# Block 2's projections with tokens on partitions in 512-column products, and a fixed time per product in the ordering estimate

## The chip, the core and the metric

The kernel runs on one core of one Trainium2 chip. The metric is the device time of one execution in microseconds; of three runs of the kernel before the median is 1619.11 us (1617.6 to 1622.94). Everything is in float32: a product of two matrices is either taken in full float32, or both operands are split into a leading part (type float32r) and the rest, and three products of the parts are added.

## The reference

Two blocks follow each other on 256 tokens of width 1024.

```
x = first_block(x, mem, ...)      # mixer (conv + chunked recurrence), cross attention, 16-expert MoE, final norm
for l in range(2):                # second_block, on the tokens x and on 256 context tokens
    h, hc = modulated_norm(x), modulated_norm(ctx)
    na_q, na_k, na_v, cq, ckv, k_rope, dq, dk, dv, z, gm = split(h @ w_in[l])      # and the same of hc
    na_q, na_k, dq, dk = rms_norm per head of 64 columns          # dq, dk rotated afterwards
    mq = rms_norm(cq) @ w_uq[l];  k_nope, mv = split(rms_norm(ckv) @ w_ukv[l])
    o_na, o_mla, o_diff = three attentions
    y = sum_i sigmoid(g_i) * ((o_i * silu(z_i)) @ w_br[l][i])
    x = x + gate * (y @ w_out[l])                                 # ctx likewise, in layer 0 alone
```

## The kernel before

The program is one stream of instructions for each engine, written out by a planner in Python. Every part of the computation is a generator (a fiber); `run` always continues the fiber whose next step can begin first by an estimate of when each engine is free (`self.E`), and among equals the one of the higher priority. The estimate of a product's time is made in `_pe` (L346). What stands on an engine stands in that order for good: each engine works through its stream in order and waits where an operand isn't there. The program is built three times; each of the last two builds takes the order of the weight loads from the build before it.

Weights come in units of 1024 values a partition (512 KB) by a DMA from SP into the large tiles. ScalarE writes the leading part (`wh`, 128x1024), VectorE the rest (`wl`), and the products of a unit then use both. Names of tiles in a profile: `wh`, `wl` the split weights, `t` a fiber's tile, `p` a PSUM bank of 512 float32 columns, `csts` the constants (a product with these at L370 is a transposition), `X` the tokens. In `p<-wh,t` the weights move through TensorE and the tokens are stationary: this is a product with tokens on partitions. `p<-t,wh` is the other kind, with features on partitions.

PSUM has eight banks; `pg`, `pa`, `po` (L176) limit how many of these the products of projections, the short products and the attention outputs may hold at once: 6, 4 and 3.

Block 2 has its keys, values and queries (attention branches `na` and `diff`), the last latent keys and values (`w_ukv`) and the final matrix (`w_out`) through `gemm_t` (L679): blocks of 256 columns, the weights of a unit being four rows of 128 by 256 columns, and the two token tiles of a stream side by side in one PSUM bank. Three products for each row of 128, token tile and block:

```
self.mm(o, hi.k(k)[:, ts], w.hi[:, k - u], m == 0 and k == 0, False)
self.mm(o, hi.k(k)[:, ts], w.lo[:, k - u], False, False)
self.mm(o, lo.k(k)[:, ts], w.hi[:, k - u], False, m == 1 and k == kt - 1)
```

`ev_qk` takes keys or queries out of PSUM (square, sum per head, 1/rms once for both blocks of 256 columns, scale, rotate, transpose), `ev_vals` the values, `evac` in `out` the last product (times the gate, onto the residual, and in layer 1 out by a DMA). Block 1 has products of this kind with 512 columns already, in `gemm_x`.

In the middle of the kernel is the router of block 1's experts. Its logits are two groups of twelve short products (`t,wrh` and `t,wrl`, into 20 partitions); ScalarE copies them out (`t<-p,cols 20x256`), TensorE transposes them (`csts,t` into 20 columns), and a chain of short VectorE operations makes the routing. Near it `prepare` writes sixteen tables of the attention's bias into DRAM, by DMAs that are issued from ScalarE's own stream (L949, `toep<-in_na_rpb_dram`).

Of the kernel before, what the change touches and what calls it, by code (L numbers as in the profile page):

```python
# [26 lines left out]
# ---------------------------------------------------------------- layout of the packed small operands  # L27
# [72 lines left out]
# ---------------------------------------------------------------- program order  # L100
# [5 lines left out]
class Fiber:  # L106
# [20 lines left out]
class Tiles:  # L127
    """[128, n, w] held as tiles of per entries each."""
# [12 lines left out]
class Core:  # L141
    """Emits the program. Each part of the computation is a generator; run() interleaves them by an
    estimate of when the engines are free, so that one part's products fill another's waits."""
# [18 lines left out]
    GR, GP = 4, 0.5  # L162
# [40 lines left out]
    # ---- generators  # L203
# [47 lines left out]
    # ---- memory  # L251
# [28 lines left out]
    def alloc_t(self, n, w, dt=F32):  # L280
        """[128, n, w] in as many tiles as it takes."""
# [25 lines left out]
    def wlimit(self, phase):  # L307
        """the phase's share of the large tiles for weights; what a smaller share gives back is used once it is empty."""
# [11 lines left out]
    def soon(self, eng="pe"):  # L320
        """other parts first, if what comes would hold up the engine."""
# [16 lines left out]
    # ---- engines  # L338
# [7 lines left out]
    def _pe(self, cycles, rows, par=1.0):  # L346
        """the array runs at its full clock in a tick that follows one with enough columns; par: products side by side."""
# [5 lines left out]
        self._op("pe", cycles * (0.4167 if self.hot else 0.8333) / par)  # L353
# [8 lines left out]
    def mm(self, out, lhsT, rhs, start, stop, par=1.0):  # L362
        n, m = self._n(rhs), self._n(lhsT)
        self._pe(max(n, 2 * m) if rhs.dtype == F32R else max(4 * n, 4 * m), lhsT.shape[0], par)
# [53 lines left out]
    def rsqrt(self, ss, inv_n, n):  # L418
        """1/sqrt(ss*inv_n + EPS) for a [128, n] tile; 1/sqrt(ss) without inv_n."""
# [18 lines left out]
    def hilo(self, hi, lo, src, after=None):  # L438
        """Exact split of src: hi carries its leading bits, lo the rest."""
# [4 lines left out]
    # ---- weights  # L444
# [17 lines left out]
    def _slot(self):  # L462
        """a large tile for weights: the one that was given back first."""
# [10 lines left out]
    def _pump(self):  # L474
        """loads ahead of the products, in the recorded order, as far as the buffers allow."""
# [3 lines left out]
    def splitter(self):  # L479
        """splits ahead of the products; hi: the leading bits of the unit's weights, lo: the rest."""  # L480
# [26 lines left out]
    def wget(self, name, lead, k0, k1, c0, c1, plain=False):  # L507
        """the weights [k0*128:k1*128, c0:c1], [128, k, c]: split, or plain as they are."""
# [66 lines left out]
    def gemm_w(self, name, lead, K, c0, c1, hi, lo, evac):  # L575
        """out[feature, token]: evac(i, psum [128, 2, 256]) for each 256 columns."""
# [19 lines left out]
    def gemm_x(self, name, lead, K, c0, c1, hi, lo, evac, cw=512):  # L596
        """out[token, feature]: evac(i, [psum of tokens 0-127, psum of tokens 128-255], n)."""
# [2120 lines left out]
```

## Time and profile before

| | |
|---|---|
| three runs, median (lowest, highest) | 1619.11 us (1617.6, 1622.94) |
| profiled execution: span of its instructions | 1620.1 us |
| TensorE matmuls, busy | 1581.4 us (98%), 11642 instructions |
| TensorE weight loads, busy | 1333.1 us (82%) |
| VectorE / ScalarE / GpSimd busy | 980.5 / 753.2 / 44.1 us |
| mean granted TensorE clock | 0.995 |

The profile's page gives no time for the profiled execution beside its span; the span lies within the three runs, 1.0 us above their median. How to read the rows: a matmul's duration (about 0.28 us for 256 columns) is its way through the array, and the next one starts long before it ends. What a product costs in a row of products is the distance from one start to the next. A full-float32 product shows as two instructions.

### The profile page before, as it was taken

How to read it: one execution, taken by the hardware profiler on the slowest of the kernel's cores; microseconds unless marked ns; L12 is line 12 of the kernel's file. 1: busy time of each engine (PE TensorE's matmuls, PEld its weight loads, DVE VectorE, ACT ScalarE, POOL GpSimd, SP SyncE). 2: the span in 40 equal slices, each digit the busy share in tenths (PEclk: the TensorE clock that was granted, in tenths of full speed). 3: DMA queues.
4: the chain of work that ended last, by engine and by line, in shares of the span. 5: the costliest groups of instructions: out<-in, count | busy, mean ns of one | idle time of the engine just before them, and what ended most of it. 6: DMA issues, size and time to landing. Idle time of an engine off the chain costs nothing.

```text
span 1620.1 us, 28916 instructions
## 1 busy us (share of the span) xinstructions
PE 1581.4 (98%) x11642; PEld 1333.1 (82%) x11642; DVE 980.5 (61%) x2035; ACT 753.2 (46%) x1357; POOL 44.1 (3%) x75
## 2 busy tenths in 40 slices
PE   7999999699999999999999999999999999999998
PEld 6899899663565447998888788888999999989898
DVE  5876557522232246758675463754896776767755
ACT  5535345322522135746653345463464465546652
POOL 0000000000000001011000000000010200000000
PEclk9999999899999999999999999999999999999999
DMA  9667656779998996565314453534755425234441
GB/s 344 225 189 241 221 162 188 237 275 377 383 372 291 353 384 211 170 182 132 104 50 123 128 157 113 166 92 130 234 167 159 118 79 144 69 113 112 144 133 63
DMA packets 233175, 305.31 MB, mean 188 GB/s; under 512 B 17184, under 2 KB 160288, under 8 KB 233040
## 3 DMA queue, kind: packets, MB, share of 16 engines
q1 hardware_dynamic: 222608, 293.11, 56.5%
q0 software_dynamic: 2576, 7.77, 1.7%
q10 hardware_dynamic: 7856, 2.56, 0.8%
q8 instruction: 93, 1.52, 0.4%
q14 instruction: 42, 0.34, 0.1%
HBM read 302.34 MB, written 2.90 MB: 188 GB/s over the span
## 4 chain that ended last, share of the span: by engine, by line
PE 63%; DVE 2%; ACT 1%; DMA 1%; issue 0%; DVEq 0%; ACTq 0%
PE p L365 59%; PE p L370 4%; ACT t L378 1%; DMA w<-in_w_in_dram 1%; DVE t L388 0%; DVE wl L388 0%; DVE t L400 0%; ACT wh L378 0%; DVE t L407 0%; DVE t L409 0%; ACT X L378 0%; DVE t L395 0%; DVE t L393 0%; DVE p L388 0%; DVE X L388 0%
## 5 line engine op out<-in xcount | busy, mean ns | idle before, releaser
L365 PE MATMUL p<-t,wh 128*128 128x256 f32 (+1 forms) x2640 | 560.9, 309 | 0.7 <-DVE t L388 0.7
L365 PE MATMUL p<-wh,t 128*128 128x256 f32 (+2 forms) x2248 | 464.9, 301 | 1.5 <-ACT wh L378 1.2
L388 DVE TENSOR_TENSOR wl<-w,wh 128x1024 fp32r<-128x1024 f32 (+2 forms) x318 | 373.4, 1194 | 133.6 <-ACT wh L378 122.5
L365 PEld LDWEIGHTS p<-t,wh 128*128 128x128 f32 x2640 | 424.1, 190 | 31.0 <-issue 7.8
L378 ACT ACTIVATE t<-p 128x512 f32<-128x512 f32 (+5 forms) x381 | 193.5, 528 | 453.2 <-PE p L365 341.7
L365 PE MATMUL p<-t,wl 128*128 128x256 f32 (+1 forms) x1312 | 399.6, 305 | 0.5 <-DVE wl L388 0.5
L365 PEld LDWEIGHTS p<-wh,t 128*128 128x128 f32 x2248 | 366.3, 192 | 23.9 <-issue 11.0
L378 ACT ACTIVATE wh<-w 128x1024 fp32r<-128x1024 f32 (+2 forms) x318 | 318.7, 1031 | 42.5 <-DMA toep<-in_na_rpb_dram 11.4
L365 PE MATMUL p<-wl,t 128*128 128x256 f32 (+2 forms) x1124 | 335.4, 298 | 2.1 <-DVE wl L388 2.1
L365 PEld LDWEIGHTS p<-t,wl 128*128 128x128 f32 x1312 | 250.0, 191 | 11.8 <-DVE wl L388 0.9
L365 PE MATMUL p<-t,t 128*64 128x128 f32 (+8 forms) x1824 | 244.6, 308 | 3.0 <-DVE t L388 1.3
L365 PEld LDWEIGHTS p<-t,t 128*64 128x64 f32 (+3 forms) x1824 | 195.3, 170 | 51.6 <-issue 27.6
L365 PEld LDWEIGHTS p<-wl,t 128*128 128x128 f32 x1124 | 216.0, 192 | 7.9 <-DVE wl L388 3.0
L378 ACT ACTIVATE t<-p,t 128x512 f32<-128x512 f32 (+3 forms) x232 | 120.0, 555 | 129.7 <-PE p L365 85.6
L365 PE MATMUL p<-w,t 128*64 128x512 f32 x768 | 176.1, 598 | 1.3 <-ACT t L378 0.7
L370 PE MATMUL p<-csts,t 128*128 128x128 f32 (+1 forms) x848 | 119.4, 278 | 12.9 <-ACT t L378 11.9
L365 PEld LDWEIGHTS p<-w,t 128*64 128x64 f32 x768 | 51.4, 136 | 95.7 <-issue 87.5
L370 PEld LDWEIGHTS p<-csts,t 128*128 128x128 f32 (+1 forms) x848 | 96.0, 141 | 31.3 <-ACT t L378 15.6
L388 DVE TENSOR_TENSOR t<-t,t 128x512 f32<-128x512 f32 (+9 forms) x254 | 107.0, 455 | 15.0 <-ACT t L378 12.1
L378 ACT ACTIVATE t<-p,cols 128x256 fp32r<-128x256 f32 (+4 forms) x91 | 50.4, 604 | 127.5 <-PE p L370 74.8
L407 DVE TENSOR_REDUCE t<-p 128x1 f32<-128x512 f32 (+1 forms) x124 | 85.0, 685 | 40.3 <-PE p L365 39.0
L400 DVE SCALAR_TENSOR_TENSOR t<-t,p 128x512 f32<-128x512 f32 x70 | 47.8, 684 | 72.2 <-ACT t L378 38.8
(95 smaller groups left out, 684.8 us busy)
## 6 DMA issues: line engine op xcount, KB each, us to landing
w<-in_w_in_dram SPq DMA_DIRECT2D x206, 512.0 KB, 4.4
w<-in_w_gate_dram SPq DMA_DIRECT2D x64, 512.0 KB, 8.5
w<-in_w_up_dram SPq DMA_DIRECT2D x64, 512.0 KB, 10.3
w<-in_w_down_dram SPq DMA_DIRECT2D x64, 512.0 KB, 10.7
w<-in_w_ada_dram SPq DMA_DIRECT2D x48, 512.0 KB, 4.5
w<-in_w_out_dram SPq DMA_DIRECT2D x32, 512.0 KB, 3.9
w<-in_w_br_dram SPq DMA_DIRECT2D x28, 512.0 KB, 4.4
w<-in_w_kv_dram SPq DMA_DIRECT2D x16, 512.0 KB, 4.1
```

The costliest lines, as they stand in the source:

```text
L365: self.nc.tensor.matmul(out, lhsT, rhs, start=start, stop=stop)
L370: self.nc.tensor.transpose(out, in_, self.ident[:k, :k])
L378: self.nc.scalar.activation(out, in_, func, bias=bias, scale=scale, **kw)
L388: self._e(eng, self._n(out), False, after).tensor_tensor(out, a, b, op=op)
L400: e.scalar_tensor_tensor(out, a, s, b, op0=op0, op1=op1)
L407: e.tensor_reduce(out, a, axis=AX, op=op, negate=True)
```

## The change

Comments and docstrings are taken out as well, so that the added lines below stand four lines further down (L365 is L369 in the changed kernel), but for the later ones.

- `gemm_t` works in blocks of 512 columns. A unit of weights is two rows of 128 by 512 columns (the same 512 KB), a token tile has a whole PSUM bank, and both streams take four banks at once. With `each` the token tiles are taken out one by one.
- `ev_qk`, `ev_kv`, `heads_T`, `ev_vals` and `out`'s `evac` work on one token tile of 512 columns instead of two tiles of 256; `GR`, the number of column blocks that `out` has open at once, goes from 4 to 2 (2048 columns of PSUM in both).
- `_pe` adds a fixed time to each product in the planner's estimate: 13.5 ns for a float32r product, 6 ns for a float32 one, 3 ns for a transposition. This is in no instruction, but it moves instructions all over the program.

```
-    GR, GP = 4, 0.5
+    GR, GP = 2, 0.5
+    PEF, PEX = 13.5, 3.0
...
-        self._op("pe", cycles * (0.4167 if self.hot else 0.8333) / par)
+        self._op("pe", cycles * (0.4167 if self.hot else 0.8333) / par + fixed)
...
-    def gemm_t(self, name, lead, K, c0, c1, hi, lo, streams, evac, cw=256, base=0, kev=None, group=1):
+    def gemm_t(self, name, lead, K, c0, c1, hi, lo, streams, evac, cw=512, base=0, kev=None, group=1, each=False):
         kt = K // 128
+        ku = 1024 // cw
+        tiles = [T * (1 - s) + m * 128 - base for s in streams for m in range(2)]
...
-                ps = yield from self.palloc("pg", len(streams))
+                ps = yield from self.palloc("pg", len(tiles))
...
+                    for a, (p, t0) in enumerate(zip(ps, tiles)):
+                        ts = slice(t0, t0 + 128)
+                        for k in range(u, u1):
+                            self.mm(p[:, :cw], hi.k(k)[:, ts], w.hi[:, k - u], k == 0, False)
+                            self.mm(p[:, :cw], hi.k(k)[:, ts], w.lo[:, k - u], False, False)
+                            self.mm(p[:, :cw], lo.k(k)[:, ts], w.hi[:, k - u], False, k == kt - 1)
+                        if u1 == kt and each:
+                            evs.append(self.spawn(evac((c - c0) // cw, a, p), ...))
...
         def ev_qk(streams, gcol, dst, tab):
-            sh = yield from sums(2, ns * 8)
+            n = 2 * len(streams)
+            def evac(_, pss):
+                ss = yield from self.alloc("T", [128, n, 8])
...
-                r = yield from roots(sh, i, 1.0 / 64)
+                r = yield from self.rsqrt(ss.rearrange("p a h -> p (a h)"), 1.0 / 64, n * 8)
...
+            def evac(i, m, ps):
+                c = slice(i * 512, i * 512 + 512)
+                tmp = yield from self.alloc("S", [128, 512])
+                self.tt(tmp, ps, g[:, c])
+                self.free(ps)
+                self.tt(res[m][:, c], tmp, res[m][:, c], OP.add)
```

The last column blocks of the final matrix on TensorE, layer 1. Before, `t_17093` and `t_17094` are the leading part and the rest of two rows of 128 of the merged branches, and `p_17097`, `p_17098` two blocks of 256 columns; each token tile has half a bank:

```order
L365 MATMUL p_17097<-wh_17154,t_17093 128x256
L365 MATMUL p_17097<-wl_17155,t_17093 128x256
L365 MATMUL p_17097<-wh_17154,t_17094 128x256
L365 MATMUL p_17098<-wh_17186,t_17072 128x256
L365 MATMUL p_17098<-wl_17187,t_17072 128x256
L365 MATMUL p_17098<-wh_17186,t_17073 128x256
```

And of the change, where `p_15660` and `p_15661` are the two token tiles of one block of 512 columns:

```order
L369 MATMUL p_15660<-wh_15714,t_15657 128x512
L369 MATMUL p_15660<-wl_15715,t_15657 128x512
L369 MATMUL p_15660<-wh_15714,t_15658 128x512
L369 MATMUL p_15661<-wh_15714,t_15657 128x512
L369 MATMUL p_15661<-wl_15715,t_15657 128x512
L369 MATMUL p_15661<-wh_15714,t_15658 128x512
```

Three products of 512 columns stand where two times three of 256 stood. Over the whole program TensorE's stream loses 2880 products of 256 columns (1920 with `wh`, 960 with `wl`) and gains 1440 of 512 (960 and 480); no other product changes in number.

ScalarE around the router's logits. Before (`p_3172`, `p_3182` are the last transposed tokens, `p_3064` the logits):

```order
L378 ACTIVATE t_3014<-p_3172,cols 128x256 x2
L378 ACTIVATE t_3014<-p_3182,cols 128x256 x2
L378 ACTIVATE t_3083<-t_3087 128x1024
L378 ACTIVATE t_2980<-p_3090 128x2x256
L949 DMA toep_2807<-in_na_rpb_dram 7x64x64 x5
L378 ACTIVATE t_3212<-p_3064,cols 20x256
L378 ACTIVATE t_3084<-t_3215 128x1024
L378 ACTIVATE wh_3248<-w_2876 128x1024
```

Of the change (`p_3009`, `p_3018` and `p_2928` are the same things):

```order
L382 ACTIVATE t_2926<-p_3009,cols 128x256 x2
L382 ACTIVATE t_2926<-p_3018,cols 128x256 x2
L956 DMA toep_2810<-in_na_rpb_dram 7x64x64 x6
L382 ACTIVATE t_2944<-t_2977 128x1024
L382 ACTIVATE wh_3053<-w_2778 128x1024
L382 ACTIVATE wh_3083<-w_2804 128x1024
L382 ACTIVATE t_3089<-p_2928,cols 20x256
L382 ACTIVATE t_3097<-t_3097 128x8
```

Six of the table's DMAs instead of five stand ahead of the logits' copy, and three long operations have come between them and it.

TensorE at the same place. Before, 24 products of 256 columns (here the first and the last three) fill the time before the logits' transposition (`csts,t_3212`):

```order
L365 MATMUL p_3064<-t_3014,wrl 20x256
L365 MATMUL p_3220<-wh_3120,t_2589 128x256
L365 MATMUL p_3220<-wl_3121,t_2589 128x256
L365 MATMUL p_3220<-wh_3120,t_2591 128x256
...
L370 MATMUL p_3245<-csts,t_3212 128x20 x2
L365 MATMUL p_3220<-wh_3169,t_2590 128x256
```

Of the change, twelve products of 512 columns (the last three here) stand ahead of the second group of logits' products, and nothing between these and the transposition:

```order
L369 MATMUL p_2958<-wh_2991,t_2589 128x512
L369 MATMUL p_2958<-wl_2992,t_2589 128x512
L369 MATMUL p_2958<-wh_2991,t_2591 128x512
L369 MATMUL p_2928<-t_2926,wrh 20x256
...
L374 MATMUL p_3091<-csts,t_3089 128x20 x2
L374 MATMUL p_3111<-csts,t_3041 128x128 x4
```

The filling work has moved from behind the logits' products to ahead of them.

## Rows read from the trace of the kernel before

**Rows 1.** The page's first part: engine, busy us (share), instructions.

```profile
PE 1581.4 (98%) x11642; PEld 1333.1 (82%) x11642; DVE 980.5 (61%) x2035; ACT 753.2 (46%) x1357; POOL 44.1 (3%) x75
```

**Rows 2.** TensorE's waits: us in total, times, longest.

```profile
PE p L370 <- ACT t L378: 11.9, 5, 8.9
PE p L365 <- DVE t L393: 11.0, 1, 11.0
PE p L365 <- DVE wl L388: 2.6, 6, 1.2
```

**Rows 3.** Timeline, TensorE, layer 1: start, us, engine, line, instruction, count.

```profile
1164.13 0.40 PE L365 MATMUL p<-wh,t 128*128 128x256 f32 x2
...
1164.49 0.40 PE L365 MATMUL p<-wh,t 128*128 128x256 f32 x2
```

**Rows 4.** Timeline, TensorE, block 1's 512-column products of both kinds.

```profile
160.20 0.62 PE L365 MATMUL p<-wh,t 128*128 128x512 f32 x2
...
160.88 0.62 PE L365 MATMUL p<-wh,t 128*128 128x512 f32 x2
...
834.45 0.62 PE L365 MATMUL p<-t,wh 128*128 128x512 f32 x2
...
835.14 0.62 PE L365 MATMUL p<-t,wh 128*128 128x512 f32 x2
```

**Rows 5.** Timeline, TensorE, a change from one kind of product to another.

```profile
472.33 0.28 PE L365 MATMUL p<-wh,t 128*128 128x256 f32 x1
472.54 1.94 PE L365 MATMUL p<-w,t 128*64 128x512 f32 x8
```

**Rows 6.** Timeline at the router, in brackets the idle time before and who ended it.

```profile
292.07 1.04 PE L370 MATMUL p<-csts,t 128*128 128x128 f32 x8
292.71 1.57 ACT L378 ACTIVATE t<-p,cols 128x256 fp32r<-128x256 f32 x4 [2.92 <-PE p L370]
294.51 0.76 ACTq L949 DMA_DIRECT2D toep<-in_na_rpb_dram  x1
295.85 11.09 ACTq L949 DMA_DIRECT2D toep<-in_na_rpb_dram  x4
306.99 0.46 ACT L378 ACTIVATE t<-p,cols 20x256 f32<-20x256 f32 x1 [11.28 <-DMA toep<-in_na_rpb_dram]
307.36 1.04 ACT L378 ACTIVATE t<-t 128x1024 fp32r<-128x1024 f32 x1
307.51 0.40 PE L370 MATMUL p<-csts,t 20*128 20x20 f32 x2 [8.93 <-ACT t L378]
...
309.07 0.63 PE L365 MATMUL p<-wh,t 128*128 128x256 f32 x2
309.71 0.63 PE L365 MATMUL p<-wh,t 128*128 128x256 f32 x2
...
322.24 1.18 PE L365 MATMUL p<-t,csts 128*128 128x16 f32 x10
```

**Rows 7.** Busy us (PE, PEld, DVE, ACT, POOL), clock, DMA share, GB/s of stretches.

```profile
300.00:312.00 12.00, 4.49 (x25) 4.45 (x26) 3.58 (x11) 2.47 (x4) 0.00 (x0) 0.57 0.70 209
400.00:500.00 100.00, 100.00 (x621) 58.61 (x617) 32.47 (x63) 36.37 (x82) 0.00 (x0) 1.00 1.03 368
```

**Rows 8.** The bias tables' DMAs: shortest/median/longest issue in ns.

```profile
L949 ACTq DMA_DIRECT2D toep<-in_na_rpb_dram x16: 755/807/5102, 242.6 to 304.5; - x16
```

**Rows 9.** VectorE by shape: count, busy us, mean ns, idle before.

```profile
L407 DVE TENSOR_REDUCE t<-p 128x1 f32<-128x512 f32 x96 | 65.9, 686 | 27.0 <-PE p L365 25.9
L388 DVE TENSOR_TENSOR t<-p,t 128x512 f32<-128x512 f32 x46 | 30.2, 686 | 16.1 <-PE p L365 14.7 <-DVE t L400 0.5
L400 DVE SCALAR_TENSOR_TENSOR t<-t,t 128x16 f32<-128x16 f32 x108 | 18.9, 175 | 3.7
```

**Rows 10.** Timeline of the end.

```profile
1615.27 0.69 DVE L388 TENSOR_TENSOR t<-p,t 128x512 f32<-128x512 f32 x1 [1.39 <-PE p L365]
1615.99 0.76 DVE L388 TENSOR_TENSOR X<-t,X 128x256 f32<-128x256 f32 x2
```

More of the change, by code (lines that the diff above doesn't have):

```diff
@@ L344, in _op, with _pe @@
         return end
-    def _pe(self, cycles, rows, par=1.0):
+    def _pe(self, cycles, rows, par=1.0, fixed=3.0):
         tick = max(self.E["pe"], self.cur.ready()) // 3413.33
@@ L363, in mm @@
         n, m = self._n(rhs), self._n(lhsT)
[L364 removed]
+        if rhs.dtype == F32R:
+            self._pe(max(n, 2 * m), lhsT.shape[0], par, self.PEF)
+        else:
+            self._pe(max(4 * n, 4 * m), lhsT.shape[0], par, 2 * self.PEX)
         self.nc.tensor.matmul(out, lhsT, rhs, start=start, stop=stop)
@@ L686, in gemm_t @@
             for _ in range(group):
-                ps = yield from self.palloc("pg", len(streams))
-                pss.append(ps if len(streams) > 1 else [ps])
-            for u in range(0, kt, 4):
-                u1 = min(kt, u + 4)
+                ps = yield from self.palloc("pg", len(tiles))
+                pss.append(ps)
+            for u in range(0, kt, ku):
+                u1 = min(kt, u + ku)
                 for i, ps in enumerate(pss):
@@ L1884, in evac @@
                     self.free(pss[a])
                     raws.append(rw)
-                drop(sh)
+                self.free(ss, r)
                 yield
-                for a, s in enumerate(streams):
-                    rw = raws[a]
+                for a in range(n):
+                    rw, s, m = raws[a], streams[a // 2], a % 2
                     turn = tab is not None and s == 0
                     if turn:
-                        yield from rope(rw, tabs[tab], 4, 64)
-                    yield from heads_T(lambda m, j: rw[:, m, 2 * j:2 * j + 2].rearrange("p h d -> p (h d)"), 128, 2,
-                                       dst[s], 2 * i, 1.0 if turn else gcol)
+                        yield from rope(rw[:, None], tabs[tab][:, :, m:m + 1], 8, 64)
+                    yield from heads_T(lambda j: rw[:, 2 * j:2 * j + 2].rearrange("p h d -> p (h d)"), 128, m,
+                                       dst[s], 1.0 if turn else gcol)
@@ L1898, in ev_vals, with evac @@
         def ev_vals(streams, v):
-            def evac(i, pss):
-                for a, s in enumerate(streams):
-                    self.act(v[s].kk(0, 2)[:, :, i * 256:i * 256 + 256], pss[a].rearrange("p (m c) -> p m c", m=2))
-                    self.free(pss[a])
-                    yield
+            def evac(_, a, ps):
+                self.act(v[streams[a // 2]].k(a % 2), ps)
+                self.free(ps)
+                yield
             return evac
@@ L1910, in keys @@
                 k[s] = yield from heads(gk.split("_")[0])
-            ev = yield from ev_qk(streams, self.colv(gk, l), k, gk if rot else None)
+            ev = ev_qk(streams, self.colv(gk, l), k, gk if rot else None)
             evs = yield from self.gemm_t(W, (l,), D, ck, ck + 512, hi, lo, streams, ev)
@@ L1914, in keys @@
                 v[s] = yield from self.alloc_t(2, 512)
-            evs += yield from self.gemm_t(W, (l,), D, cv, cv + 512, hi, lo, streams, ev_vals(streams, v))
+            evs += yield from self.gemm_t(W, (l,), D, cv, cv + 512, hi, lo, streams, ev_vals(streams, v), each=True)
             return k, v, evs
@@ L1921, in queries @@
                 q[s] = yield from heads(gq.split("_")[0])
-            ev = yield from ev_qk(streams, self.colv(gq, l), q, gq if rot else None)
+            ev = ev_qk(streams, self.colv(gq, l), q, gq if rot else None)
             evs = yield from self.gemm_t(W, (l,), D, cq, cq + 512, hi, lo, streams, ev)
@@ L2032, in ev_kv @@
                     self.free(pss[a])
                     raws.append(rw)
-                self.free(rr)
-                drop(shk)
+                self.free(rr, ss, r)
                 yield
-                for a, s in enumerate(both):
-                    rw = raws[a]
-                    yield from heads_T(lambda m, j: rw[:, m, j], 96, 2, k[s], 2 * c, self.colv("mla_k_col", 2 * l + s))
+                for a in range(4):
+                    rw, s = raws[a], both[a // 2]
+                    yield from heads_T(lambda j: rw[:, j], 96, a % 2, k[s], self.colv("mla_k_col", 2 * l + s))
```

124 lines of the change are left out of this document (47 added, 77 removed).

## The prediction

> **What bounds the kernel now.** I read the page's first part, TensorE's waits, the timeline of its products, and then the one place where it waits long. TensorE's matmuls are busy for 98% of the span and VectorE, the next engine, for 61% [rows 1]. The share alone would not prove that TensorE is the bound, since a matmul's record lasts longer than the distance to the next. The waits do: the twelve rows of the view add up to 33.6 us, and two places hold 20 us of these, one wait of 11.0 us at the start and one of 8.9 us at the router [rows 2]. Everywhere else the next product starts when the array is free. So time is won where products get cheaper, and lost where the new order makes TensorE wait.
>
> The cost of a product is its pitch, the distance between starts. Products of 256 columns come in threes every 0.36 us (1164.13 to 1164.49) [rows 3], 120 ns each. Products of 512 columns are in the kernel already, in block 1: of the kind that the change makes, three every 0.68 us (160.20 to 160.88), 227 ns each; of the kind with features on partitions three every 0.69 us (834.45 to 835.14) [rows 4].
>
> **The products.** The order counts 2880 products of 256 columns less and 1440 of 512 columns more; that is 480 times three wide ones for 960 times three narrow ones. Each saves 2 x 0.36 - 0.68 = 0.04 us, so 480 x 0.04 = 19.2 us. With the other kind's 0.69 us it would be 480 x 0.03 = 14.4 us. I take 19.2, as these rows are the same product: tokens stationary, split weights moving, units of two rows of 128 by 512. Half as many stationary loads go with it; these lie beside the products and are in the pitch already.
>
> The Trainium skill, "TensorE: Matmul & The Clock Gate", section "Back-to-back issue gap", gives N/2.4 ns plus 2.5 ns for a warm product of N columns. By that the change would save 1440 x 2.5 ns = 3.6 us (an estimate from the page). The rows differ: 120 ns is 13.3 ns above 256/2.4, and 227 ns is 13.7 above 512/2.4 [rows 3, 4], so here the measurement decides; what is left of the page's case is a rival below.
>
> **Changes between kinds of products.** Going over from split weights to full float32 costs time: the next product starts 0.21 us later (472.33 to 472.54) instead of 0.12 [rows 5]. The new order has 679 stretches of one kind instead of 652. Some such changes cost nothing, so 27 more cost between 0 and 27 x 0.09 = 2.4 us; I take +1.0.
>
> **The router.** This is the one place where I can see a long wait change. Before, the last transposed tokens come at 292.07, ScalarE issues five of the bias tables' DMAs from 294.51 to 306.94 (295.85 + 11.09), and only then copies the logits out, at 306.99; TensorE stands for 8.93 us [rows 6]. The issues themselves hold ScalarE up, up to 5.1 us for one where 0.8 is the median [rows 8]. In the new order six stand there. The four that are merged into one row took 11.09 us; counting one of them as quick (0.76) leaves 3.4 us for each that had to wait, so a sixth makes 12.43 + 3.4, less the 0.6 us in which a copy stood between the first and the second: 15.3 us. Behind the DMAs, three long operations (1.04 us each [rows 6]) now stand ahead of the logits' copy: 3.1 us. With the same start of 2.4 us after the transpositions the copy begins 2.4 + 15.3 + 3.1 = 20.8 us after them, against 306.99 - 292.07 = 14.9 before. TensorE's fill is the same (12 x 0.227 = 2.7 us now, 24 x 0.12 = 2.9 before), merely moved ahead of the logits' products. So its wait grows by 5.9 us, to about 15. Behind TensorE, the routing, and with it the experts' products, is late by as much.
>
> Some of it comes back. Between the logits' transposition (307.51) and the next step of the routing (322.24), 14.7 us pass for 72 products and the transposition, which at full pace take 8.64 + 0.3: 5.8 us too many. A part is the clock: it was at 0.57 of full speed, that is mostly its lower level of 1.2 GHz, in 300 to 312 [rows 7], behind the wait, and three products took 0.64 us instead of 0.36 (309.07 to 309.71 [rows 6]). The rest is waiting for weights, whose splits stood behind the routing's chain on VectorE and ScalarE. In the new order that chain has one split of weights or tokens in it where three stood, and the products need the later splits only behind it. I leave the slow clock (about 1.6 us) and drop the rest, -4.2 us. Net: +1.7. Bounds: all six DMAs at the median of 0.81 us would bring the copy 4.5 us earlier than before, with the 4.2 us in all -8.7; four held up for 5.1 us each cost 6.6 us more than my 15.3, and with nothing coming back that is +12.5. I take +1.7, since the group there [rows 6] is the one that stands at the same place.
>
> **PSUM.** In one place both streams go through `gemm_t` for keys and then values (layer 1, branch `diff`). The keys now take four banks at once, and the values ask for four more of the six. They get them when two of the keys' banks have been read out: a square, four sums of 0.69 us, eleven short operations of 0.175 us and two scalings of 0.69 us [rows 9], with 0.6 us for the first square 6.7 us. In the new order some 7 us of short products of the attention stand between. The wait lies between 0 and 6.7 us; I take +1.0, near the covered end.
>
> **Beside the experts' weights.** 48 of the 480 wide threes stand among the experts' products, where the DMA engines run at a share of 1.03 [rows 7]. There 48 x 0.04 = 1.9 us may turn into waiting for weights; I take half, +1.0. Bytes loaded stay the same.
>
> **What costs nothing.** Copies out of PSUM are fewer and wider (64 ScalarE operations of 128 columns become 32 of 256, for one); VectorE and ScalarE are 61% and 46% busy [rows 1], so this stands beside TensorE's work, and would cost only if the copies were late (rival 3). The end is the same: the last product, then 0.69 us for the gate and 0.76 us for the sum [rows 10], which becomes one operation of 512 columns, then a DMA of the same 256 KB. The start is the same on TensorE up to the first wide products, so its 11.0 us wait stays.
>
> **Sum.** -19.2 + 1.0 + 1.7 + 1.0 + 1.0 = -14.5 us on the profiled span of 1620.1: 1605.6. That execution lies 1.0 us above the runs' median, so 1604.6, rounded 1605 us. Own range 1598 to 1612: 3 us either way for the moved order elsewhere, where all waits outside the two long ones came to 33.6 - 19.9 = 14 us before [rows 2], and about 4 for the router.
>
> **Rivals.**
> 1. The router's wait goes away. The tables' DMAs are issued quickly, as most were [rows 8]. Against it: more of them in one go than before, and the last group was slow. With -8.7 instead of +1.7: 1594 (1590 to 1598).
> 2. The router eats most of it. Four of the six are held up for 5 us, and the late weights stay: +12.5 instead of +1.7, 1615 (1612 to 1620). For it: one issue of 5.1 us [rows 8]. Against: the group at this place took 3.4 for each.
> 3. Slower than before: the copies of keys and queries come too late. Before, the sums of the first 256 columns ran while TensorE was on the second; now nothing of a block can begin before all of its products are done. The chain of one stream's block is 0.6 + 2 x 0.69 + 11 x 0.175 + 2 x 0.69 = 5.3 us [rows 9] ahead of the transpositions, and there are 13 such blocks. From four exposed ones on (21 us) the gain is gone; eight would give 1605 + 42 = 1647, five 1631. Against: at the places that I looked at, 48 wide products (10.9 us) or more stand between a block and its transpositions, and before only 14 us of all waits lay outside the two long ones.
> 4. The wide product in block 2 costs nearly twice the narrow one: if its fixed part were as small against two narrow ones as 2.5 ns, 15.6 us of the gain would be missing, 1620, no change. The rows speak against it [rows 4]. The page's rule named above would give this.
> 5. The products are not fewer than they look: the counted order rules that out, 0.01.
>
> **How the numbers follow.** The forecast 0.61; rival 1 0.15; rival 2 0.13; rival 3 0.06; rival 4 0.04; rival 5 0.01. No change means within 0.3%, 4.9 us, about what a measurement of this kernel can tell: 1614.3 to 1624.0. Faster: 0.61 + 0.15 + 0.07 of rival 2 = 0.83. Same: 0.06 of rival 2, rivals 4 and 5: 0.11. Slower: 0.06. The range of 1593 to 1617 leaves out 0.05 of rival 1, 0.03 of rival 2, and rivals 3 to 5 (0.11), about 0.19.
>
> **What would show it.** In the changed profile: 512-column threes with 0.68 us between starts in layers 0 and 1, and no 256-column products with moving weights; about 10200 matmul records; at the router a wait of ScalarE for the tables of some 15 us and of TensorE for ScalarE of about 15; behind it, 0.64 us threes for some 3 us and then no waits for `wl` before the next routing step; a short wait of TensorE in layer 1 between keys and values, for VectorE. I am wrong if the 512-column pitch in block 2 is 0.70 us or more, if TensorE's waits outside start and router grow past 20 us, or if the router's wait is under 6 or over 25 us.

## The result, and the profile after

The changed kernel takes 1629.5 us (median of four runs, 1628.4 to 1630.7), against 1620.5 us for the kernel before on the same chip (four runs, 1617.6 to 1622.9). The ratio is 1.0055, interval [1.0043, 1.0068]: slower by 9 us, where 1605 us was forecast. The profiled execution has a span of 1628.3 us, 8.2 us more than before. Of run 12 below, one of four executions took 3940.65 us, more than twice the others (1590.4 to 1593.9) for no reason on record; that run's time is the median of these three.

The first part of the page of the kernel after, as [rows 1]:

```profile
PE 1569.7 (96%) x10202; PEld 1259.0 (77%) x10202; DVE 976.9 (60%) x1995; ACT 748.8 (46%) x1321; POOL 42.2 (3%) x75
```

There are 1440 products fewer and TensorE is busy for 11.7 us less, yet the span is longer. So the time lies between products. TensorE's waits in the kernel after, as [rows 2] (us in total, times, longest):

```profile
PE p L374 <- ACT t L382: 16.6, 4, 15.2
PE p L369 <- DVE sil L416: 10.6, 1, 10.6
PE p L374 <- DVE t L392: 8.6, 4, 6.0
PE p L374 <- DVE t L397: 5.7, 1, 5.7
PE p L369 <- DVE t L392: 5.1, 4, 2.8
PE p L369 <- DVE wl L392: 4.8, 5, 2.0
...
```

All rows of this view add up to 53.4 us (33.6 before). Without the start (10.6) and the router (15.2) that is 27.6 us, against 13.7 before. Three waits are new: 6.0 us for a block's scaled columns (L392), 5.7 us for a row norm (L397), and 2.8 us, put down to that line as well.

**The wide products cost what was forecast.** Layer 1, TensorE, in the kernel after (start, us, engine, line, instruction):

```profile
1196.40 0.39 PE L369 MATMUL p<-wl,t 128*128 128x512 f32 x1
...
1197.08 0.39 PE L369 MATMUL p<-wl,t 128*128 128x512 f32 x1
```

From one three to the next, 0.68 us, as [rows 4] had it for block 1.

**The router went as forecast too.** The same place as [rows 6], in the kernel after:

```profile
286.07 1.03 PE L374 MATMUL p<-csts,t 128*128 128x128 f32 x8
...
288.35 14.93 ACTq L956 DMA_DIRECT2D toep<-in_na_rpb_dram  x5
303.33 1.06 ACT L382 ACTIVATE t<-t 128x1024 fp32r<-128x1024 f32 x1 [15.01 <-DMA toep<-in_na_rpb_dram]
304.29 1.99 ACT L382 ACTIVATE wh<-w 128x1024 fp32r<-128x1024 f32 x2
306.19 0.45 ACT L382 ACTIVATE t<-p,cols 20x256 f32<-20x256 f32 x1
306.69 1.44 PE L374 MATMUL p<-csts,t 20*128 20x20 f32 x6 [15.16 <-ACT t L382]
```

The logits' copy starts 20.1 us behind the last transposed tokens (20.8 forecast), and TensorE stands for 15.2 us (about 15 forecast).

**Where the time went.** To see the loss by place, I took for every product the time from its start to the next one's start, less the usual distance for that pair of kinds (the median, for changes of kind the lower quarter). What is left is time lost to waits and to the slow clock. Each column is one profiled execution (spans of 1620.1, 1628.3, 1642.3 and 1630.8 us). The usual distances add up to 1523.7 us before and 1505.3 after: 18.4 us gained. The rest, by stretch, in us (the last two columns are experiments told of below):

| stretch (us of the kernel after) | before | after | wide blocks alone | fixed times alone |
|---|---|---|---|---|
| start, to 280 | 11.9 | 13.8 | 12.0 | 11.4 |
| router, 280 to 340 | 17.6 | 17.6 | 24.4 | 14.6 |
| experts, 340 to 620 | 20.9 | 18.3 | 17.2 | 17.6 |
| layer 0, 620 to 735 | 1.2 | 2.7 | 6.7 | 3.0 |
| layer 0, 735 to 790 | 4.8 | 9.6 | 6.2 | 2.6 |
| layer 0, 790 to 1195 | 13.4 | 14.7 | 15.0 | 17.5 |
| between the layers, 1195 to 1235 | 0.1 | 8.7 | 8.7 | 9.0 |
| keys and values of `diff`, 1235 to 1345 | 0.5 | 11.6 | 7.4 | 2.6 |
| rest of layer 1 | 10.0 | 10.0 | 25.7 | 12.7 |
| sum | 80.4 | 107.0 | 123.3 | 91.0 |

26.6 us are lost and 18.4 gained, 8.2 net, as the spans have it. Of the loss 24.5 us lie at three places.

**Between the layers.** Layer 1 begins with the row norm of the residual stream. VectorE's last sum of that stream, the norm's first operation, and TensorE's transpositions of the normed rows, in the kernel after:

```profile
1190.84 0.69 DVE L392 TENSOR_TENSOR X<-t,X 128x512 f32<-128x512 f32 x1
...
1213.62 1.22 DVE L406 SCALAR_TENSOR_TENSOR t<-X 128x1024 f32<-128x1024 f32 x1
...
1217.94 3.70 PE L374 MATMUL p<-csts,t 128*128 128x128 f32 x16 [5.75 <-DVE t L397]
```

The norm's input is complete at 1191.5, and the norm begins 22 us later; its 4 us then stand before TensorE with nothing beside them. In the kernel before, the norm begins right behind the last sum:

```profile
1194.75 0.76 DVE L388 TENSOR_TENSOR X<-t,X 128x256 f32<-128x256 f32 x2
1195.54 1.23 DVE L402 SCALAR_TENSOR_TENSOR t<-X 128x1024 f32<-128x1024 f32 x1
```

No operand holds the norm back in the kernel after: it is the order in which the program is written (run 2).

**Keys and values of `diff` in layer 1.** The wide products of the keys (both streams, four token tiles) end at 1295.2. TensorE and VectorE behind them:

```profile
1295.15 1.09 PE L369 MATMUL p<-t,t 128*64 128x128 f32 x16
1296.18 1.09 PE L374 MATMUL p<-csts,t 128*128 128x128 f32 x8
1297.20 3.85 PE L369 MATMUL p<-t,t 64*128 64x256 f32 x34
1307.02 1.09 PE L374 MATMUL p<-csts,t 128*128 128x128 f32 x4 [5.97 <-DVE t L392]
...
1296.50 2.46 DVE L413 TENSOR_REDUCE t<-t 128x8 f32<-128x512 f32 x4 [5.39 <-ACT t L382]
1298.88 1.21 DVE L392 TENSOR_TENSOR wl<-w,wh 128x1024 fp32r<-128x1024 f32 x1
...
1306.18 2.48 DVE L392 TENSOR_TENSOR t<-p,t 128x512 f32<-128x512 f32 x4
```

No projection stands there: the values ask for four PSUM banks, four of the six are the keys', and these come free one by one with the scalings of the last row, from 1306.8 on. The transposition at 1307.02 is the first scaled tile's. Between the sums and the roots VectorE has 4.8 us of other work (a split of weights, a bias, the attention's maxima, 1298.88 to 1303.7). TensorE has 58 instructions of short products, 5.9 us, and then waits.

**Layer 0, 757 us.** A third wait, at a block of one stream (TensorE, then VectorE, kernel after):

```profile
757.12 2.17 PE L369 MATMUL p<-t,t 128*64 128x128 f32 x24
759.60 2.49 PE L374 MATMUL p<-csts,t 128*128 128x128 f32 x16 [0.31 <-ACT t L382]
764.86 3.68 PE L369 MATMUL p<-t,t 128*64 128x128 f32 x32 [2.77 <-DVE t L392]
...
764.02 1.29 DVE L392 TENSOR_TENSOR t<-p,t 128x512 f32<-128x512 f32 x2
```

The product at 764.86 belongs to the attention. Both its operands are copies that ScalarE had made by about 763.0. In the program it writes into the PSUM bank of the block's own first token tile, and it waits for the first of the two scalings (764.02), which is the last operation to read that bank. So this is a wait for a bank, too.

**The clock adds to each wait.** The three stretches in the kernel after (us of the stretch, busy us of PE, PEld, DVE, ACT, POOL, granted clock, DMA share, GB/s):

```profile
1211.00:1226.00 15.00, 9.00 (x41) 7.14 (x40) 10.74 (x25) 9.72 (x17) 0.00 (x0) 0.77 0.26 79
1300.00:1325.00 25.00, 19.03 (x119) 15.29 (x115) 21.08 (x53) 11.26 (x24) 0.00 (x0) 0.80 0.13 38
757.00:772.00 15.00, 11.91 (x94) 10.08 (x94) 12.36 (x32) 9.54 (x19) 0.59 (x1) 0.77 0.32 87
```

The clock is at its lower level for a part of each. In the kernel before, the stretches around the same places have it at 1.00:

```profile
1175.00:1215.00 40.00, 40.00 (x338) 40.00 (x338) 36.38 (x70) 24.63 (x36) 6.16 (x12) 1.00 0.58 169
1255.00:1290.00 35.00, 34.88 (x294) 33.80 (x292) 25.59 (x50) 16.97 (x28) 9.97 (x17) 1.00 0.52 142
750.00:780.00 30.00, 29.09 (x260) 27.08 (x259) 24.50 (x62) 19.90 (x40) 3.28 (x5) 1.00 0.49 117
```

So 6.0 us of wait at 1301 cost 11.6 us with what follows it, and 5.9 between the layers 8.7.

### The profile page after: what moved, and what is told of

Its sections match the earlier page's. It is cut to its first block, busy times and chain, and to the rows that moved or that the text cites. A ratio compares the mean times of both kernels' runs of the same rounds, so it can differ in the third digit from the quotient of the medians.

```text
span 1628.3 us, 25938 instructions
## 1 busy us (share of the span) xinstructions
PE 1569.7 (96%) x10202; PEld 1259.0 (77%) x10202; DVE 976.9 (60%) x1995; ACT 748.8 (46%) x1321; POOL 42.2 (3%) x75
## 4 chain that ended last, share of the span: by engine, by line
PE 89%; DVE 6%; ACT 2%; DMA 1%; SPq 1%; ACTq 1%; issue 1%; DVEq 0%
PE p L369 83%; PE p L374 6%; DVE wl L392 1%; DVE t L392 1%; ACT t L382 1%; DVE t L404 1%; SPq L458 1%; DMA w<-in_w_in_dram 1%; ACTq L956 1%; DVE t L411 1%; DMA w<-in_w_gate_dram 1%; ACT wh L382 0%; DVE t L397 0%; DVE t L413 0%; DVE t L399 0%
## 5 line engine op out<-in xcount | busy, mean ns | idle before, releaser
L369 PE MATMUL p<-t,wh 128*128 128x256 f32 (+1 forms) x2640 | 564.4, 310 | 0.9 <-DVE t L392 0.6
L392 DVE TENSOR_TENSOR wl<-w,wh 128x1024 fp32r<-128x1024 f32 (+3 forms) x314 | 370.7, 1202 | 146.5 <-ACT wh L382 137.0
L369 PEld LDWEIGHTS p<-t,wh 128*128 128x128 f32 x2640 | 426.9, 191 | 34.1 <-issue 8.9
L369 PE MATMUL p<-wh,t 128*128 128x512 f32 (+1 forms) x1288 | 414.5, 393 | 1.8 <-DVE t L392 1.7
L369 PE MATMUL p<-t,wl 128*128 128x256 f32 (+1 forms) x1312 | 400.8, 306 | 4.4 <-DVE wl L392 4.4
L382 ACT ACTIVATE wh<-w 128x1024 fp32r<-128x1024 f32 (+3 forms) x314 | 316.3, 1041 | 22.9 <-DMA w<-in_w_in_dram 8.4
L369 PEld LDWEIGHTS p<-wh,t 128*128 128x128 f32 x1288 | 242.5, 189 | 60.9 <-issue 10.9
L369 PEld LDWEIGHTS p<-t,wl 128*128 128x128 f32 x1312 | 251.2, 191 | 16.0 <-DVE wl L392 5.2
L369 PE MATMUL p<-wl,t 128*128 128x512 f32 (+1 forms) x644 | 250.6, 389 | 0.5 <-DVE wl L392 0.4
L369 PE MATMUL p<-t,t 128*64 128x128 f32 (+8 forms) x1824 | 246.8, 311 | 4.4 <-DVE t L392 2.8
L369 PEld LDWEIGHTS p<-t,t 128*128 128x128 f32 (+3 forms) x1824 | 197.3, 172 | 52.4 <-issue 29.3
L382 ACT ACTIVATE t<-p,t 128x512 f32<-128x512 f32 (+2 forms) x200 | 115.1, 595 | 136.9 <-PE p L369 97.1
L369 PE MATMUL p<-w,t 128*64 128x512 f32 x768 | 175.8, 598 | 0.0
L374 PE MATMUL p<-csts,t 128*128 128x128 f32 (+1 forms) x848 | 126.1, 284 | 31.1 <-ACT t L382 16.6
L374 PEld LDWEIGHTS p<-csts,t 128*128 128x128 f32 (+1 forms) x848 | 99.6, 143 | 55.7 <-ACT t L382 24.3
L369 PEld LDWEIGHTS p<-wl,t 128*128 128x128 f32 x644 | 121.7, 189 | 23.5 <-DVE wl L392 1.5
L392 DVE TENSOR_TENSOR t<-t,t 128x512 f32<-128x512 f32 (+9 forms) x226 | 106.5, 498 | 28.3 <-ACT t L382 25.4
L369 PEld LDWEIGHTS p<-w,t 128*64 128x64 f32 x768 | 50.8, 136 | 93.1 <-issue 86.3
```

Source lines behind the costliest of these rows:

```text
L369: self.nc.tensor.matmul(out, lhsT, rhs, start=start, stop=stop)
L374: self.nc.tensor.transpose(out, in_, self.ident[:k, :k])
L382: self.nc.scalar.activation(out, in_, func, bias=bias, scale=scale, **kw)
L392: self._e(eng, self._n(out), False, after).tensor_tensor(out, a, b, op=op)
```

## The experiments

Three theories. A: two new waits in layer 1, one for PSUM banks, one for a row norm written late, make up most of the loss. B: the third rival on record, the chains of keys and queries come too late everywhere. C: the fixed product times in the planner's estimate did the harm. Each run was compared with the kernel before on the same chip, whose median lay between 1620.5 and 1622.0 us; times are medians, ratios stand against before.

**1. Values ahead of keys** (only where both streams go through at once):

```
-            evs = yield from self.gemm_t(W, (l,), D, ck, ck + 512, hi, lo, streams, ev)
+            evs = []
+            if len(streams) == 1:
+                evs += yield from self.gemm_t(W, (l,), D, ck, ck + 512, hi, lo, streams, ev)
             for s in streams:
                 v[s] = yield from self.alloc_t(2, 512)
             evs += yield from self.gemm_t(W, (l,), D, cv, cv + 512, hi, lo, streams, ev_vals(streams, v), each=True)
+            if len(streams) > 1:
+                evs += yield from self.gemm_t(W, (l,), D, ck, ck + 512, hi, lo, streams, ev)
```

> The kernel after, with one edit: where both streams go through keys and values (layer 1, branch diff), the values' block runs ahead of the keys' block. Theory A (two new waits in layer 1): one of them is the wait for PSUM banks at 1300 us, where the values ask for four banks while the keys hold four of six; values let go of their banks one by one, so the 6.0 us wait at 1300.77 and the slow clock behind it (4.3 us) go, about 10 us: 1619 us (1616 to 1623), with the wait at 1211.9 unchanged. Theory B (the third rival of the prediction, chains of keys and queries come too late in most of the 13 blocks): the keys' chain now ends later still, nothing is gained: 1629 us (1627 to 1634). Theory C (the fixed product times of the ordering estimate did the harm, not the width): 1629 us as well.

Measured: 1616.8 us, ratio 0.9968 [0.9956, 0.998], 12.6 us less than the kernel after. The place, and the later place where the keys' sums, roots and scalings stand now (1338.8 to 1345):

```profile
1270.00:1320.00 50.00, 50.00 (x334) 41.13 (x333) 31.11 (x67) 31.84 (x67) 5.65 (x9) 1.00 0.34 84
...
1318.00:1348.00 30.00, 30.00 (x194) 24.27 (x193) 15.05 (x34) 16.69 (x31) 0.00 (x0) 1.00 0.37 106
```

TensorE is busy throughout at full clock. What follows the keys now is a block of queries that asks for two banks, and the 9.5 us up to the transposition of the first scaled tile (1338.3 to 1347.8) are filled with products. The keys' chain has the same instructions, but none of VectorE's other work stands in its middle any more: 6.4 us from the last product to the first scaled tile, where it was 11.7. So the edit gave it more cover and made it shorter, and the run doesn't tell the two apart. That the order of the two blocks makes this wait, as theory A has it, is shown; B forecast no gain here.

**2. The norm written early** (the first two lines stand behind the sum in `evac` of `out`):

```
+                if l == 0 and s == 0:
+                    self.set(self.xdone[2 * i + m])
...
         def rest():
-            yield from self.wait(first)
+            yield from self.wait(*self.xdone)
             yield from self.hidden(self.X, 1, 0, hi, lo)
             self.set(x1)
+            yield from self.wait(first)
             yield from self.wlimit("l1")
```

> The kernel after, with one edit in what the ordering waits for: the row norm of the residual stream between layer 0 and layer 1 may be written as soon as the four sums of the last projection are written, instead of when the part of the program that wrote them has had its next turn. Theory A: the norm's first operation, 22 us behind the last sum now (1191.5 to 1213.6), starts within 3 us of it; the 5.9 us wait at 1211.9 and the slow clock behind it (2.2 us) go: 1621 us (1618 to 1625), with the wait at 1300 unchanged in length. Theory B: 1629 us (1627 to 1632), as no chain of keys or queries is touched. Theory C: 1629 us.

Measured: 1617.0 us, ratio 0.9982 [0.9972, 0.9991], 12.5 us less. VectorE at the place:

```profile
1191.51 0.69 DVE L392 TENSOR_TENSOR X<-t,X 128x512 f32<-128x512 f32 x1
...
1193.25 1.22 DVE L406 SCALAR_TENSOR_TENSOR t<-X 128x1024 f32<-128x1024 f32 x1
```

The norm starts 1.05 us behind the last sum, and of the 8.7 us lost between the layers 0.5 are left. The other 4 us of the gain came unasked, from the order that follows: 3 of them at the keys of `diff`, though the wait there still lasts 6.0 us. Before the edit, the norm had to wait for the part of the program that holds layer 0's last projection to come to its end. That part has the same priority as layer 1's projections and a later number, so by the planner's rule it gets no turn while layer 1 has a product ready. The kernel before has the same rule; that there layer 1 had none ready at that moment is a guess from its order, which no run shows.

**3. Both edits:**

> The kernel after with the edits of the two runs before it together. Theory A: the two waits are independent and both go: 1629.5 - 10 - 8 = 1611 us (1607 to 1616), and TensorE has no wait over 4 us behind the router. Theory B: new waits for keys' and queries' copies take their place, 1625 to 1632 us. Theory C: 1625 to 1632 us.

Measured: 1608.5 us, ratio 0.992 [0.9904, 0.9937]: 21 us less than the kernel after, and 12 less than before. TensorE's waits:

```profile
PE p L374 <- ACT t L382: 15.1, 3, 14.6
PE p L369 <- DVE sil L416: 10.6, 1, 10.6
PE p L369 <- DVE wl L392: 5.0, 4, 2.4
PE p L369 <- DVE t L392: 4.9, 3, 2.8
...
```

Behind the router none is over 2.8 us. With these two waits gone the gain of the products is there, less the wait at 762 and the like.

**4. The wide blocks alone** (`PEF, PEX = 0.0, 0.0`, and 0 for transpositions):

> The wide blocks of the kernel after, with the fixed product times of the ordering estimate set to zero again, for all products and transpositions, so the estimate is that of the kernel before. Theory A: the wait for PSUM banks comes from the width and stays (about 10 us of the 28 us lost); the late norm may go or stay, as it hangs on which part is written next; 1620 us (1612 to 1628). Theory B: the chains stay as long as they were: 1629 us or more. Theory C: the gain of the products comes out whole: 1605 us (1600 to 1610).

Measured: 1641.2 us, ratio 1.0123 [1.0106, 1.014]. Theory C is refuted, and its opposite is the case: with wide blocks the fixed times are worth 11.7 us. No theory had the number, as A left the rest of the order unchanged. The table above shows the loss spread: 6.8 us more at the router, 15.7 more in the rest of layer 1. The late norm costs 8.7 us here as well.

**5. The fixed times alone** (256 columns, `_pe` and `mm` as in the kernel after):

> The kernel before, 256-column blocks, with the fixed product times of the kernel after in its ordering estimate and nothing else. Theory D (an estimate nearer to the real product times gives a better order at either width): with wide blocks the fixed times are worth 1641.2 - 1629.5 = 11.7 us, so 1620.5 - 11.7 = 1609 us (1605 to 1613). Theory E (what such a table of costs does is a matter of which piece falls where): the order before had few waits outside start and router (14 us), there is little to win and more to lose: 1624 us (1614 to 1636).

Measured: 1635.8 us, ratio 1.0093 [1.0075, 1.0111], at the far end of theory E; D is refuted. The same fixed times that help wide blocks by 11.7 us harm narrow ones by some 15 us (by the ratio). The largest piece is the boundary again, VectorE:

```profile
1186.14 0.76 DVE L392 TENSOR_TENSOR X<-t,X 128x256 f32<-128x256 f32 x2
1214.75 0.76 DVE L392 TENSOR_TENSOR X<-t,X 128x256 f32<-128x256 f32 x2
```

Here layer 0's last sum itself comes 29 us behind the one ahead of it. So the late norm is no matter of width: every order tried without the second edit loses 8.7 to 9.1 us there, save those of the kernel before and of run 10 below, which stays close to it.

**6. Narrow keys and queries in the kernel after** (`gemm_t`, `ev_qk` and `heads_T` of the kernel before for these two):

> The kernel after, with the blocks of keys and queries of the branches na and diff in 256 columns again (their projections, sums, scalings and transpositions as in the kernel before); values, latent projections and the output projection stay wide. 14 blocks of one stream, 2 x 8 threes each, are narrow again: 224 x 0.04 = 9 us more of products. Theory A (two new waits in layer 1): both stay. The keys' two narrow halves hold four PSUM banks until both sums are there, and the values' wide block still asks for four; nothing is changed about the late norm. 1629.5 + 9 = 1638 us (1631 to 1645). Theory B (chains of keys and queries too late): these chains are now as in the kernel before, so the 28 us of new waits go: 1629.5 + 9 - 25 = 1613 us (1608 to 1620).

Measured: 1627.6 us, ratio 1.0042 [1.0027, 1.0056]. Neither number was met. The products cost 8.5 us more by their usual distances, as said. The late norm stays (9.1 us). At the keys of `diff` 7.7 us are lost instead of 11.6, and at 735 to 790 us 2.3 instead of 9.6. So B has a share: with the narrow chains some 11 us go at two places, though the order is another one there, too; it is not the 25 us of theory B, and not the boundary.

**7. The tables' DMAs on GpSimd**, on top of both edits (`nc.scalar.dma_start` to `nc.gpsimd.dma_start`):

> The kernel with both edits (1608.5 us), with the bias tables' 16 DMAs issued by GpSimd instead of ScalarE. ScalarE's six issues between the last transposition and the logits' copy at the router (15 us) are gone; the copy is held up only by the start of 2.4 us and three operations of 1.04 us, against 2.7 us of products: TensorE's wait falls from 14.5 us to 3, and some of it comes back as waiting for weights. Theory F (the router's wait is the tables' issues): 1598 us (1595 to 1602). Theory G (the chain of the routing on VectorE is the next bound, so what is won ahead of the logits is lost behind them): 1605 us (1602 to 1609).

Measured: 1605.4 us, ratio 0.99 [0.9881, 0.9919], a step of 3 us from run 3, whose interval overlaps. Theory G's number came for another reason. The router's wait is gone (17.2 us lost there in run 3, 7.7 here), but a new one stands at 244. ScalarE and TensorE:

```profile
243.55 0.34 ACT L382 ACTIVATE wrh<-t 128x160 fp32r<-128x160 f32 x1 [5.06 <-DMA t<-in_wr_dram]
...
244.42 4.11 PE L369 MATMUL p<-t,t 128*128 128x256 f32 x10 [3.17 <-ACT t L382]
```

ScalarE waits for the router's weights, asked for right behind the burst of tables, and TensorE for ScalarE.

**8. The wide blocks alone, with both edits:**

> The wide blocks without the fixed product times (1641.2 us), with both edits, values first and norm early. The trace of the wide blocks alone shows the same two waits, 5.9 us at 1215 and 4.3 us at 1300. Theory A: both go with the slow clock behind them, 1641 - 18 = 1623 us (1617 to 1629); what is left above the kernel with both edits and the fixed times (1608.5) is what the fixed times are worth, spread over smaller waits. Theory H (without the fixed times the order is so off that other waits take the place of these): 1633 us or more.

Measured: 1628.3 us, ratio 1.0041 [1.0029, 1.0053]: 13 us less, within theory A's range, near its end. The boundary's 8.7 us went to 0.2 and the keys' place from 7.4 to 4.0; the rest of layer 1 still lost 21.5 us (25.7 without the edits). With the edits in both, the fixed times are worth 20 us.

**9. The router's weights and the rows of lambda on GpSimd too, ahead of the tables:**

> The kernel with both edits and the tables on GpSimd (1605.4 us), with two more loads moved from ScalarE's queue to GpSimd's, ahead of the tables: the router's weights and the rows of lambda. In the run before, the tables left in a burst from 225 to 238 us, the router's weights were asked for at 237.4, and ScalarE waited 5.06 us for them, TensorE 3.2 us behind it, with a slow clock after that (4.9 us over the usual pitch, against none in the kernel with both edits alone). Theory J (that wait is the whole of what the router's 11 us were given back for): 1605.4 - 3.2 - 4.2 = 1598 us (1595 to 1601). Theory G (what is won at the router is lost behind it): 1604 us (1602 to 1607).

Measured: 1597.1 us, ratio 0.9858 [0.9837, 0.9879], within 1 us of theory J. TensorE waits 0.56 us for the logits instead of 14.6.

**10. The same three loads moved in the kernel before:**

> The kernel before, with the same loads (tables, router's weights, rows of lambda) issued by GpSimd instead of ScalarE, nothing else. It tells how much of the gain of the last run against the kernel before has to do with the wide blocks. TensorE's wait at the router (8.9 us) goes but for about 2 us, and the slow clock behind it (1.6 us): 1620.5 - 8 = 1612 us (1609 to 1616). If the bursts of the tables hold up the weights instead: 1618 to 1623 us.

Measured: 1613.0 us, ratio 0.9951 [0.9933, 0.997]: 8 us less, as expected. So of the 24 us by which run 9 beats the kernel before, 8 are to be had without wide blocks, and 16 belong to these with the two edits, if the gains add up.

**11. Values one stream after the other, order kept:**

```
-            evs += yield from self.gemm_t(W, (l,), D, cv, cv + 512, hi, lo, streams, ev_vals(streams, v), each=True)
+            for s in streams:
+                evs += yield from self.gemm_t(W, (l,), D, cv, cv + 512, hi, lo, [s], ev_vals([s], v), each=True)
```

> The kernel after, with the order of keys and values kept, and the values of layer 1's branch diff projected one stream after the other: each stream asks for two PSUM banks instead of four at once, and two of the six are free while the keys hold four. The four units of weights are loaded and split twice; the number of products is the same. Theory A (banks): the first stream's 48 products (10.9 us) can run at once behind the keys' products, the wait of 6.0 us at 1300.77 falls to 3 or less with most of the slow clock behind it: 1629.5 - 7 = 1622 us (1618 to 1626). Theory B (the keys' chain itself is too late, whatever the banks): 1629 us (1627 to 1633).

Measured: 1624.8 us, ratio 1.002 [1.001, 1.0031]: 4.7 us less, at the weak end of theory A, but not by its means: the wait is 4.9 us, where 3 or less was expected, and by the reckoning of the table only about 2 us of the gain lie at this place, and as much at the start, which the edit doesn't touch. TensorE, VectorE and ScalarE:

```profile
1299.25 0.39 PE L369 MATMUL p<-wh,t 128*128 128x512 f32 x1
1304.52 1.76 PE L369 MATMUL p<-t,t 128*64 128x128 f32 x14 [4.88 <-DVE t L392]
...
1303.78 2.48 DVE L392 TENSOR_TENSOR t<-p,t 128x512 f32<-128x512 f32 x4
...
1293.44 3.20 ACT L382 ACTIVATE t<-p 128x512 f32<-128x512 f32 x7
```

With two banks the values do start at once, but only one unit of them (12 products, to 1299.6) is written there. Then comes a product of the attention. Both its operands are copies of ScalarE, made by 1296.6. It writes into the bank of the keys' first token tile, and waits for the first of the four scalings (1303.78), the last operation to read that bank. All eight banks are taken then: four by the keys, two by the values, two by scores of the attention. So the wait is again for a bank that the keys hold, and what sets its length is when VectorE comes to the scalings, behind the four tiles' sums and roots and 4.8 us of other work between these (1296.5 to 1301.3).

**12. One large tile more for intermediates in layer 0**, on top of run 9 (`"l0": (4, 3)` to `(3, 3)`):

> The best kernel so far (both edits, router's loads on GpSimd, 1597.1 us), with one large tile of SBUF less for loaded weights in layer 0, so one more for its intermediates (30 instead of 29). It is aimed at the third new wait of the wide kernels, 2.8 us at 762 with 0.4 us at 759 and the slow clock behind them, about 6 us. Theory K (layer 0's next projection stands there for want of a large tile, so TensorE has only a block's transpositions and what follows from them to do): the wait goes, 1597 - 6 + 0 to 4 for one weight less in advance: 1593 us (1590 to 1597). Theory B (there the chain of the queries' block is simply too long for what can be put beside it): the wait stays, 1597 to 1602 us.

Measured: 1591.5 us, ratio 0.9811 [0.9776, 0.9845], the lowest of all: 38 us under the kernel after. The interval overlaps that of run 9, so the last step is not clear of the noise. The number is theory K's, the reason only in part: a wait stays at the place, shortened from 2.8 to 2.0 us (3 us less lost from 735 to 790), 3 us were won from 790 to 905 and 2.5 lost again behind that. TensorE:

```profile
758.66 0.63 PE L374 MATMUL p<-csts,t 128*128 128x128 f32 x4 [2.03 <-DVE t L392]
```

## Why the prediction was wrong, step by step

- **The bound and the price of the products: right.** TensorE is the bound. -19.2 us of products and +1.0 of changes between kinds, 18.2 together, stand against 18.4 found. Rival 4 is out: 0.68 us for three is 227 ns for a product, 13.7 above 512/2.4. The Trainium skill, "TensorE: Matmul & The Clock Gate", section "Back-to-back issue gap", gives 2.5 ns there for an isolated product, which the prediction put on a row of them; the measurement decides.
- **The router: right.** A wait of 15.2 us was found where about 15 was said, and the whole stretch lost as much as before (17.6 us, +1.7 forecast): what was forecast to come back behind the wait came back. So neither rival 1 nor rival 2. Run 10's 8 us shows that this wait is a cost of the kernel before, too.
- **The experts' weights: +1.0 forecast**, 2.6 us won instead. Small; its cause stays open.
- **"PSUM ... I take +1.0, near the covered end": the first failed step.** It cost 11.1 us (0.5 to 11.6). The place and the mechanism were named, with two numbers wrong and one missing. The chain from the last wide product to the first scaled tile took 11.7 us (1295.15 to 1306.8), and 12.3 to the second, where I had 6.7, since VectorE had 4.8 us of other work in the middle of it; I had added up the chain's own instructions as if VectorE were theirs alone. The cover was 5.9 us instead of 7. And the bounds of 0 to 6.7 left out the slow clock behind a wait, though [rows 7] show it and the router's term prices it. The chain's 11.7 us and 0.2 to the next product's start, less the cover of 5.9, are the 6.0 measured; the clock and smaller waits behind it make up the rest. Runs 1 and 3 take it all away. I had also counted banks at this one place, and for the values alone: in run 11 and at 757 it is a short product of the attention that waits for a bank.
- **"3 us either way for the moved order elsewhere": the second failed step, and the larger.** Outside router and PSUM the moved order cost 8.6 us between the layers and 4.8 at 757, with 1 to 2 at three more stretches. I had taken the size of the small waits before as the measure of what a new order may do. Runs 4, 5 and 8 show the real measure: for the same products, a change in the estimate alone moved the time by -12 (run 4), +15 (run 5) and -20 us (run 8 against run 3), as much as the products can give. The late norm could have been read from the order, by the 25 other instructions of VectorE between the last sum and the norm, where there were none before; I had compared the orders at three other places.
- **Rival 3 (copies too late, chance 0.06): the right side for a part of the reason.** Two of the 13 chains became exposed, and by run 6 some 11 us of the loss go back to that. What counts beside the length of a chain is whether the next products have their banks to run beside it: in run 1 the chain of four tiles is fully hidden. The remaining 9 us, between the layers, are no rival's on record.
- **What would have shown it wrong** was named: waits outside start and router over 20 us. They are 27.6.
- **The whole miss**, 22.7 us on the span (1605.6 forecast, 1628.3 measured): 10.1 too little for PSUM, 8.6 between the layers, 4.8 at 757, 4.7 at three smaller stretches; the experts' weights, the router and the products gave back 3.6, 1.7 and 0.2.

What stays open: why only some of the chains lost their cover, and what in the wide blocks alone costs 15.7 us in the rest of layer 1. There the order is another one throughout, and I did not take it apart.

## What to carry to other kernels

When an edit also moves the order, the products' gain is the sure part and the order's part can be as large with either sign; so walk every point where all work must pass through one chain (a norm between layers, a router, the first use of a block) in both orders, and look for what TensorE has beside it. Price a wait with VectorE's other work in the chain, and with the slow clock behind it: 5.9 us cost 8.7 here, and 6.0 cost 11.6. When blocks grow, count what the next block asks for at once (four banks of six, with four held), and what the short products beside it ask for (in run 11 all eight were held), for a chain that was hidden by these is exposed as soon as they can't start.

## What the runs showed of the hardware

- Issuing the tables' DMAs cost ScalarE 0.755 us at the least and 5.2 at the most in the kernel after (five in a row held it for 15.0 us); the same 16 from GpSimd took 0.83 to 0.87 us each in run 9, and none was held up.
- Behind fourteen such issues in 12 us a small load came late: the router's weights kept ScalarE waiting for 5.06 us in run 7, and for 0.82 us in run 3, where ScalarE had asked for them at the same time (237.5) without the burst ahead of it.
